# Seven quarter products in place of eight in twenty MLP blocks of a decoder layer, with the MLP input normalised first and the residual kept in HBM

## The chip, the core and the metric

The kernel runs on one NeuronCore of a Trainium2 chip. A core has five engines with a queue each: TensorE (PE in the profile; its weight loads are PEld), VectorE (DVE), ScalarE (ACT), GpSimd (POOL) and SyncE (SP), which here only issues DMAs. Each engine runs its queue in order; semaphores tie the queues together. The metric is the device time of one execution in microseconds (us).

## What is computed

One inference step of a hybrid decoder layer: a token mixer (gated linear attention and retention), a cross-attention into 256 memory tokens, and a squared-ReLU MLP, each between two RMSNorms and added to the residual. There are 576 tokens (512 of a prompt, 64 of samples), the width is 1024, the MLP's hidden width 4096, and all is in 32-bit floats. What the change touches is the end of `layer`:

```python
x = x + rmsnorm(cross_attn(rmsnorm(x, g_pre_xa), mem_k, mem_v, w_xq, w_xo), g_post_xa)
hf = rmsnorm(x, g_pre_ffn)
x = x + rmsnorm(jnp.square(jax.nn.relu(hf @ w_up)) @ w_down, g_post_ffn)
```

## The kernel before

Activations lie transposed: features on the 128 partitions (8 tiles of 128 for the width, `KT`), tokens along the free dimension, 576 columns (`NT`) in two halves of 288 (`NH`). A 32-bit product is made of three matmuls in the fp32r type (`mm3`): every operand is split into a rounded high part and the rest (`split`: an ACT cast for the high part, a DVE subtraction for the rest; `split_p` has the subtraction on POOL). So each matmul of 128 x 128 weights against 288 columns stands three times: high weight by high input, rest by high, high by rest.

Weights come from HBM in tiles of 128 x 1024 (512 KB, one output tile of 128 features). `plan` lists them in the order of use; `wfetch` issues the next DMA on SP into one of four `wraw` buffers, `wsplit` makes `wh` and `wl` of it (three buffers each), `wnext` hands out a split tile and keeps two ahead. `gemm_m` takes one tile through both halves (48 matmuls) into a PSUM tile of `psg` (two buffers).

The MLP runs in four groups `g` of 1024 hidden features. An up stage (eight `gemm_m`) gives the hidden features, which ACT (relu), DVE (square) and a split turn into the operand `xh`, `xl` of the down stage (eight more), whose sums collect in `y3` on DVE. In group 0's up stage and in group 3's down stage the halves run one after the other (`project`), and four of the eight weight tiles are kept from the first half to the second (`KEEP_FFN`), so that two are loaded again.

What stands around: `chain_xa` ends the cross-attention. As a generator it goes on by one step at each `tick`, between the matmuls of a `project`: `residual` norms the projection, adds it into `res` (which stays in SBUF to the end) and writes `res` times the gain, split, to `bh`, `bl`. The MLP's input is thus not yet divided by its root mean square; its statistics (`vff`) enter only at the end, in `rstd` of the last `residual`, which adds the MLP's normed output to `res` and stores it to `y_out`. The order on each engine is that of the built program; a scheduler places the instructions of the generators and of neighbouring stages.

```python
for g in range(4):
    ...
        for k in range(KT):
            to_h(h2(hh[:, k, :]), h2(hl[:, k, :]), gemm_m(fh, fl))
    ...
        for k in range(KT):
            ps = gemm_m(hh, hl)
            ...
                nc.vector.tensor_tensor(out=h2(y3[:, k, :]), in0=ps, in1=h2(y3[:, k, :]), op=ALU.add)
```

Of the kernel before, what the change touches and what calls it, by code (L numbers as in the profile page):

```python
# [56 lines left out]
def decoder_step(ctx, tc, xT, memT, ktc, vc, s_gla, s_ret, w_in, w_ga, w_a2, w_mix, w_xq, w_xk, w_xv, w_xo,  # L57
                 w_up, w_down, vecs, cst, gam, y_out, mk_out, mv_out, sg_p, sr_p, sg_s, sr_s):
# [20 lines left out]
    vff = [[perm.tile([96, 3], F32, name=f"vff{i}{j}") for j in range(2)] for i in range(2)]  # L79
# [5 lines left out]
    wz = acta.tile([P, 256], F32R, name="wz")  # L85
# [75 lines left out]
    for g in range(4):  # L161
        plan += keep(whole(w_up), KEEP_FFN) + rest(whole(w_up), KEEP_FFN) if g == 0 else whole(w_up, 4 * g)
        plan += keep(whole(w_down, 12), KEEP_FFN) + rest(whole(w_down, 12), KEEP_FFN) if g == 3 else whole(w_down, 4 * g)
    raws, ready, staying = [], [], []

    def wfetch():
        if plan:
            src, mode = plan.pop(0), RING
            if isinstance(src, tuple):
                src, mode = src  # L170
            raw = wp.tile([P, 1024], F32, name="wraw", bufs=N_RAW)
            nc.sync.dma_start(out=raw if len(src.shape) == 2 else raw.rearrange("p (k n) -> p k n", n=src.shape[2]), in_=src)
# [29 lines left out]
    def gemm(ps, w, xh, xl, c, k0=0, k1=KT):  # L202

        wh, wl = w
        for k in range(k0, k1):
            mm3(ps, wh[:, k, :], wl[:, k, :], xh[:, k, c], xl[:, k, c], k == 0, k == KT - 1)

    def gemm_m(xh, xl):
# [5 lines left out]
        return ps[:, :, :NH]  # L214

# [152 lines left out]
    y2p = ctx.enter_context(tc.tile_pool(name="y2p", bufs=1))  # L368
# [51 lines left out]
    def residual(y, r, half, ss, ss2=None, g2=None, oh=None, ol=None, scale=None, done=None):  # L420

        c = hc(half)
        rs, dg = rstd(ss, 3, 96, scale)
        yield
        bc = bcast(dg, 3, 96)
        for j in range(4):
# [81 lines left out]
    fh = actb.tile([P, KT, NT], F32R, name="bh")  # L508
    fl = actb.tile([P, KT, NT], F32R, name="bl")

    def chain_xa(half):

        ss2 = y2p.tile([P, 2, 384], F32, name="ss2")
        yield from residual((y2a, y2b)[half], rr, half, ss[half], ss2[:, :, :NH], V_PRE_FFN, fh, fl)

        def stats():
            yield
            nc.vector.reciprocal(vff[half][0], meansq(ss2[:, :, :NH], 3, 96))
            nc.vector.tensor_tensor(out=vff[half][1], in0=vff[half][0], in1=vff[half][0], op=ALU.mult)
        yield from stats()  # L520

    side.append(chain_xa(0))
    project(ah, al, 1, to(y2b, V_POST_XA, ss[1]))
    drain()
    side.append(chain_xa(1))


    hp = ctx.enter_context(tc.tile_pool(name="hp", bufs=2))
    staying.append(ctx.enter_context(tc.tile_pool(name="keepf", bufs=KEEP_FFN)))
    y3 = None  # L530
    for g in range(4):
        hh = acta.tile([P, KT, NT], F32R, name="xh")
        hl = acta.tile([P, KT, NT], F32R, name="xl")

        def to_h(hv, lv, ps):
            r = hp.tile([P, 2, NH], F32, name="hr")
            nc.scalar.activation(r, ps, AF.Relu)  # L537
            nc.vector.tensor_tensor(out=r, in0=r, in1=r, op=ALU.mult)  # L538
            split(hv, lv, r)

        if g == 0:
            for half in range(2):
                c = hc(half)
                project(fh, fl, half, lambda b, ps, first: to_h(hh[:, 2 * b:2 * b + 2, c], hl[:, 2 * b:2 * b + 2, c], ps), keep=KEEP_FFN)
                drain()
        else:
            for k in range(KT):
                to_h(h2(hh[:, k, :]), h2(hl[:, k, :]), gemm_m(fh, fl))
        if g == 0:
            y3 = biga.tile([P, KT, NT], F32, name="y3", tag="biga")  # L550
        if g < 3:
            for k in range(KT):
                ps = gemm_m(hh, hl)
                if g == 0:
                    nc.scalar.copy(h2(y3[:, k, :]), ps)
                else:
                    nc.vector.tensor_tensor(out=h2(y3[:, k, :]), in0=ps, in1=h2(y3[:, k, :]), op=ALU.add)  # L557

    def last(half):
# [672 lines left out]
```

## Time and profile before

| | |
|---|---|
| median of 3 runs (lowest, highest) | 1225.04 us (1223.53, 1228.98) |
| the profiled execution | 1223.69 us, its span 1222.0 us |
| busy share of the span | PE 98%, DVE 57%, ACT 43%, POOL 13% |
| matmuls | 9194 |
| mean granted TensorE clock | 0.991 of 2.4 GHz |

The span reaches from the first to the last instruction. A matmul's record lasts about 0.3 us, but they are pipelined: the step from one to the next is what counts. Idle time of an engine that nobody waits for costs nothing. Waits are given with the instruction that ended them, under its engine, its line in the kernel and the tile it writes and reads.

### The profile page before, as it was taken

How to read it: one execution, taken by the hardware profiler on the slowest of the kernel's cores; microseconds unless marked ns; L12 is line 12 of the kernel's file. 1: busy time of each engine (PE TensorE's matmuls, PEld its weight loads, DVE VectorE, ACT ScalarE, POOL GpSimd, SP SyncE). 2: the span in 40 equal slices, each digit the busy share in tenths (PEclk: the TensorE clock that was granted, in tenths of full speed). 3: DMA queues.
4: the chain of work that ended last, by engine and by line, in shares of the span. 5: the costliest groups of instructions: out<-in, count | busy, mean ns of one | idle time of the engine just before them, and what ended most of it. 6: DMA issues, size and time to landing. Idle time of an engine off the chain costs nothing.

```text
span 1222.0 us, 22137 instructions
## 1 busy us (share of the span) xinstructions
PE 1193.4 (98%) x9194; PEld 1170.8 (96%) x9194; DVE 692.9 (57%) x1217; ACT 527.9 (43%) x944; POOL 155.2 (13%) x156
## 2 busy tenths in 40 slices
PE   8999999999999999999999999999999999999995
PEld 8999999999999999999999777999999999999995
DVE  6757667566757675768576443783224324333544
ACT  6634556544544354535564444653223213213431
POOL 1521213121312231221001000000000000000000
PEclk9999999999999999999999999999999999999997
DMA  8753423242424242423644767442222222222401
GB/s 278 242 177 103 124 82 116 86 126 87 125 72 128 84 126 71 141 86 112 207 150 135 247 218 242 155 139 70 86 73 84 87 87 86 75 82 87 139 11 67
DMA packets 60372, 149.45 MB, mean 122 GB/s; under 512 B 5520, under 2 KB 30224, under 8 KB 60144
## 3 DMA queue, kind: packets, MB, share of 16 engines
q1 hardware_dynamic: 60272, 148.04, 37.9%
q8 instruction: 72, 1.18, 0.4%
q14 instruction: 28, 0.23, 0.1%
HBM read 134.12 MB, written 13.89 MB: 121 GB/s over the span
## 4 chain that ended last, share of the span: by engine, by line
PE 93%; DMA 2%; ACT 2%; DVE 2%; issue 1%; POOL 0%; SPq 0%; POOLq 0%; DVEq 0%; ACTq 0%
PE psg L198 27%; PE psg L200 27%; PE psg L199 27%; PE psa L198 2%; PE psa L200 1%; PE psa L199 1%; PE pso L1056 1%; DMA wraw<-in_w_xo 1%; PE psa L223 1%; ACT wh L92 1%; PE psa L773 1%; PE pso L899 1%; PE pso L900 1%; PE psa L901 1%; PE psa L776 1%; PE psa L833 1%
## 5 line engine op out<-in xcount | busy, mean ns | idle before, releaser
L198 PE MATMUL psg<-xh,wh 128*128 128x288 f32 x1808 | 537.1, 297 | 3.8 <-ACT wh L92 3.1
L199 PE MATMUL psg<-xh,wl 128*128 128x288 f32 x1808 | 533.5, 295 | 2.6 <-DVE wl L93 2.6
L200 PE MATMUL psg<-xl,wh 128*128 128x288 f32 x1808 | 532.8, 295 | 0.0
L198 PEld LDWEIGHTS psg<-xh,wh 128*128 128x128 f32 x1808 | 339.8, 188 | 6.6 <-ACT wh L92 5.1
L199 PEld LDWEIGHTS psg<-xh,wl 128*128 128x128 f32 x1808 | 340.0, 188 | 3.7 <-DVE wl L93 3.5
L200 PEld LDWEIGHTS psg<-xl,wh 128*128 128x128 f32 x1808 | 339.5, 188 | 0.8 <-DVE xl L93 0.8
L93 DVE TENSOR_TENSOR wl<-wraw,wh 128x1024 fp32r<-128x1024 f32 x189 | 233.2, 1236 | 105.2 <-ACT wh L92 104.3
L92 ACT CAST wh<-wraw 128x1024 fp32r<-128x1024 f32 x189 | 197.9, 1050 | 173.2 <-PE psg L200 122.8
L198 PE MATMUL psg<-bh,wh 128*128 128x288 f32 x640 | 189.4, 296 | 1.1 <-DMA wraw<-out_mk 1.1
L200 PE MATMUL psg<-bl,wh 128*128 128x288 f32 x640 | 188.7, 295 | 0.0
L199 PE MATMUL psg<-bh,wl 128*128 128x288 f32 x640 | 188.6, 295 | 0.0
L198 PEld LDWEIGHTS psg<-bh,wh 128*128 128x128 f32 x640 | 120.1, 188 | 1.8 <-ACT wh L92 1.3
L199 PEld LDWEIGHTS psg<-bh,wl 128*128 128x128 f32 x640 | 120.1, 188 | 0.3 <-DVE wl L93 0.2
L200 PEld LDWEIGHTS psg<-bl,wh 128*128 128x128 f32 x640 | 120.1, 188 | 0.2 <-DVE bl L93 0.2
L236 POOL TENSOR_TENSOR rs<-ms,mhalf 96x3 f32<-96x3 f32 (+1 forms) x9 | 8.9, 987 | 537.3 <-DVE ms L235 408.5
L538 DVE TENSOR_TENSOR hr<-hr 128x576 f32<-128x576 f32 x32 | 24.3, 758 | 90.0 <-ACT hr L537 90.0
L537 ACT ACTIVATE hr<-psg 128x576 f32<-128x576 f32 x32 | 20.9, 652 | 106.9 <-PE psg L200 106.9
L557 DVE TENSOR_TENSOR y<-psg,y 128x576 f32<-128x576 f32 x16 | 12.1, 758 | 62.7 <-PE psg L200 62.7
L759 ACT COPY vt<-psg 128x512 f32<-128x512 f32 x16 | 9.4, 588 | 78.0 <-PE psg L200 78.0
L688 POOL TENSOR_TENSOR rs<-mv,mhalf 128x1 f32<-128x1 f32 (+1 forms) x40 | 26.9, 672 | 108.4 <-DVE mv L683 60.7
L258 DVE TENSOR_TENSOR ss<-ss,sq 128x576 f32<-128x576 f32 x34 | 26.3, 773 | 16.8 <-ACT sq L257 16.7
L761 DVE COPY vd<-psg 128x96 f32<-128x96 f32 x32 | 6.7, 252 | 51.0 <-ACT vt L759 51.0
(274 smaller groups left out, 1605.8 us busy)
## 6 DMA issues: line engine op xcount, KB each, us to landing
wraw<-in_w_in SPq DMA_DIRECT2D x64, 512.0 KB, 3.6
wraw<-in_w_up SPq DMA_DIRECT2D x34, 512.0 KB, 3.6
wraw<-in_w_down SPq DMA_DIRECT2D x34, 512.0 KB, 3.6
wraw<-in_ktc SPq DMA_DIRECT2D x16, 512.0 KB, 4.0
wraw<-in_vc SPq DMA_DIRECT2D x16, 512.0 KB, 5.4
wraw<-in_w_xq SPq DMA_DIRECT2D x14, 512.0 KB, 4.4
wraw<-in_w_xo SPq DMA_DIRECT2D x14, 512.0 KB, 4.6
wraw<-in_w_mix SPq DMA_DIRECT2D x12, 512.0 KB, 4.5
```

Source lines behind the costliest of these rows:

```text
L92: nc.scalar.copy(hi, src)
L93: nc.vector.tensor_tensor(out=lo, in0=src, in1=f32(hi), op=ALU.subtract)
L198: nc.tensor.matmul(out, ah, bh, start=first, stop=False)
L199: nc.tensor.matmul(out, al, bh, start=False, stop=False)
L200: nc.tensor.matmul(out, ah, bl, start=False, stop=last)
L223: nc.tensor.matmul(ps[:t, i:i + 1], ss[:, l, i * t:(i + 1) * t], ones[:, 0:1], start=l == 0, stop=l == ls - 1)
L258: eng.tensor_tensor(out=ss, in0=ss, in1=sq[:, :, :n], op=ALU.add)
L537: nc.scalar.activation(r, ps, AF.Relu)
L538: nc.vector.tensor_tensor(out=r, in0=r, in1=r, op=ALU.mult)
L688: nc.gpsimd.tensor_tensor(out=rs[:t], in0=mv[:t], in1=mhalf[:t, 0:1], op=ALU.pow)
L773: nc.tensor.matmul(sc[:, :P], kf[:, ci], qf[:, ci], start=True, stop=True)
L776: nc.tensor.transpose(tp[:, P + m * P:P + (m + 1) * P], vt[:, m, ci], ident)
```

## The change

A block is two output tiles (256 features) against 1024 inputs and all 576 tokens. Groups 1 to 3 up and groups 1 and 2 down have 20 of them. Each operand is seen as 2 x 2 quarters: the weights by output tile and by even or odd input tile, the activations by even or odd input tile and by half of the tokens. Winograd's form of Strassen's scheme needs seven products of quarters (12 matmuls each) and sums of quarters ahead of and behind them. `sevenfold` issues the seven products. The sums on the output side lie in two PSUM accumulators, `acc` and the halves `b`, `c` of a `psg` tile: a product is added onto what is there, and the sum is read off in between by functions given to it (`p1`, `p5`, `u2`, `c11`, `c22`, `c12`, `c21`: ACT copies or DVE adds into `hr` for an up block, DVE adds into `y3` for a down block). The sums of weight quarters are made on POOL in `begin` (four subtractions of 128 x 512 per block), and 3.5 tiles per block are split instead of two (`unit_a` to `unit_d`; the last is the half tile `wdh`, `wdl`). The sums of activation quarters are made in `sums_f` (once, on POOL) for the up blocks and in `pairs` (one subtraction on POOL, three on DVE, for each block) for the down blocks.

For this the MLP's input is normed before it is split (`chain_xa` goes through a second `rstd`); `res` is written to `y_out` (`spill`), its SBUF room goes to `y3`, and it is read back into `res2` before the last stage. `KEEP_FFN` is gone: six tiles instead of two are loaded and split again in each of the two `project` pairs. The square of the hidden features is on ACT for the most part.

```diff
+        def unit_a():
+            pair(p0)
+            wfetch()
+        def unit_c():
+            minus(qt[:, 0], q1[:, 1], q0[:, 1])
+            pair(t)
+        def unit_b():
+            pair(p1)
+        def unit_d():
+            minus(q1[:, 0], q1[:, 0], qt[:, 0])
+            dh, dl = (wdp[0].tile([P, 512], F32R, name=n) for n in ("wdh", "wdl"))
+            split(dh, dl, q1[:, 0])
+            ready.append((dh, dl))
+        minus(qt[:, 1], q1[:, 1], q0[:, 1])
+        minus(q0[:, 1], q0[:, 1], q0[:, 0])
+        units.extend([unit_a, unit_c, unit_b, unit_d])
+        wfetch()
...
+        wa = ready.pop(0)
+        wsplit()
+        prod(acc, wa, 0, "A11", True)
+        p1(acc)
+        if raws and raws[0][1] == SEVEN:
+            begin()
+        prod(c, wa, 1, "S1", True)
+        p5(c)
+        wc = ready.pop(0)
+        prod(acc, wc, 0, "S2", False)
+        u2(acc)
+        wsplit()
+        wb = ready.pop(0)
+        prod(b, wb, 0, "A12", True)
+        c11(b)
+        prod(acc, wc, 1, "S3", False)
+        c22(acc)
+        wsplit()
+        prod(c, wb, 1, "S4", False)
+        c12(c)
+        wd = ready.pop(0)
+        if units:
+            wsplit()
+        prod(acc, wd, 0, "A22", False)
+        c21(acc)
...
+    def pairs(c1, c2, sh, sl, e1):
...
+        nc.gpsimd.tensor_tensor(out=c2[:, 0], in0=c1[:, 0], in1=c2[:, 0], op=ALU.subtract)
+        e1.tensor_tensor(out=c1[:, 0], in0=c2[:, 1], in1=c1[:, 0], op=ALU.subtract)
+        e1.tensor_tensor(out=c1[:, 1], in0=c1[:, 1], in1=c1[:, 0], op=ALU.subtract)
+        split(sh[:, 2:4], sl[:, 2:4], c2)
+        split(sh[:, 0:2], sl[:, 0:2], c1)
...
+    res2 = fsp.tile([P, KT, NT], F32, name="res2", tag="fsh")
+    for half in range(2):
+        for k in range(0, KT, 2):
+            nc.sync.dma_start(out=res2[:, k:k + 2, hc(half)], in_=y_out[:, k:k + 2, hc(half)])
```

How the rows move on an engine is shown at three places. First VectorE in the up stage of group 1, where `wl` is the rest of a weight tile and `hr`, `xl` the hidden features: before, for two of the output tiles,

```order
L538 TENSOR_TENSOR hr_11058<-hr_11058 128x576
L93 TENSOR_TENSOR wl_11126<-wraw_11003,wh_11125 128x1024
L93 TENSOR_TENSOR xl_10882<-hr_11058,xh_10881 128x576
L538 TENSOR_TENSOR hr_11118<-hr_11118 128x576
L93 TENSOR_TENSOR wl_11186<-wraw_11063,wh_11185 128x1024
L93 TENSOR_TENSOR xl_10882<-hr_11118,xh_10881 128x576
```

The same place now, from the square `c21` of one block (L740) to the sum `c12` of the next (the last L725); `fh`, `ha` and `hh` are the operands of the down stage:

```order
L740 TENSOR_TENSOR hr_11135<-hr_11135 128x288
L659 TENSOR_TENSOR hr_11135<-hr_11135 128x288
L93 TENSOR_TENSOR wdl_11277<-wraw_11054,wdh_11276 128x512
L93 TENSOR_TENSOR ha_10987<-hr_11134,ha_10987 128x2x288
L662 TENSOR_TENSOR hr_11134<-hr_11135,hr_11134 128x288
L93 TENSOR_TENSOR hl_10986<-hr_11135,hh_10985 128x2x288
L663 TENSOR_TENSOR hr_11134<-hr_11134 128x288
L93 TENSOR_TENSOR wl_11325<-wraw_11159,wh_11324 128x1024
L93 TENSOR_TENSOR hl_10986<-hr_11134,hh_10985 128x2x288
L725 TENSOR_TENSOR hr_11271<-psg_11274,hr_11271 128x288
L725 TENSOR_TENSOR hr_11272<-psa_11273,hr_11272 128x288
L93 TENSOR_TENSOR wl_11362<-wraw_11293,wh_11361 128x1024
```

Six rows for two output tiles have become fifteen: these twelve, and behind them one more L725, one `wl` and the split of `fh`.

Second VectorE in the down stage of group 1: before, for two output tiles and the next weight tile,

```order
L93 TENSOR_TENSOR wl_11478<-wraw_11363,wh_11477 128x1024
L557 TENSOR_TENSOR y3_10432<-psg_11425,y3_10432 128x576
L93 TENSOR_TENSOR wl_11534<-wraw_11419,wh_11533 128x1024
L557 TENSOR_TENSOR y3_10432<-psg_11481,y3_10432 128x576
L93 TENSOR_TENSOR wl_11590<-wraw_11475,wh_11589 128x1024
```

and now, one block, in which the third L753 is `u2`:

```order
L753 TENSOR_TENSOR y3_10483<-psa_11781,y3_10483 128x288
L93 TENSOR_TENSOR wdl_11785<-wraw_11600,wdh_11784 128x512
L753 TENSOR_TENSOR y3_10483<-psg_11782,y3_10483 128x288
L93 TENSOR_TENSOR wl_11833<-wraw_11686,wh_11832 128x1024
L753 TENSOR_TENSOR y3_10483<-psa_11781,y3_10483 128x288
L753 TENSOR_TENSOR y3_10483<-psg_11782,y3_10483 128x288
L753 TENSOR_TENSOR y3_10483<-psa_11781,y3_10483 128x288
L93 TENSOR_TENSOR wl_11866<-wraw_11801,wh_11865 128x1024
L753 TENSOR_TENSOR y3_10483<-psg_11782,y3_10483 128x288
L93 TENSOR_TENSOR wl_11883<-wraw_11718,wh_11882 128x1024
L753 TENSOR_TENSOR y3_10483<-psa_11781,y3_10483 128x288
```

Two sums read off PSUM have become seven, and the rest of the next block's first weight tile (`wl_11833`) stands ahead of `u2`.

Third GpSimd, which before had nothing in these groups; now, in one up block of group 1, with the subtractions of two weight blocks (`wraw_11156` is the buffer of sums):

```order
L212 TENSOR_TENSOR wraw_10933<-wraw_10933,wraw_11019 128x512
L212 TENSOR_TENSOR wraw_11156<-wraw_11054,wraw_11022 128x512
L212 TENSOR_TENSOR wraw_11022<-wraw_11022 128x512
L661 TENSOR_TENSOR hr_10989<-hr_10988,hr_10989 128x288
L212 TENSOR_TENSOR wraw_11156<-wraw_11054,wraw_11022 128x512
L212 TENSOR_TENSOR wraw_11054<-wraw_11054,wraw_11156 128x512
```

The first and the last row here are `unit_d` of two consecutive blocks. `unit_d` overwrites half of a tile that `unit_b` splits, so it waits for that tile's `wl` on VectorE.

## Rows read from the trace of the kernel before

**Rows 1.** The page, part 1: busy us (share) and instructions of each engine.

```profile
PE 1193.4 (98%) x9194; PEld 1170.8 (96%) x9194; DVE 692.9 (57%) x1217; ACT 527.9 (43%) x944; POOL 155.2 (13%) x156
```

**Rows 2.** The page, part 4: the chain that ended last, shares by engine.

```profile
PE 93%; DMA 2%; ACT 2%; DVE 2%; issue 1%; POOL 0%; SPq 0%; POOLq 0%; DVEq 0%; ACTq 0%
```

**Rows 3.** Windows: length, busy PE, PEld, DVE, ACT, POOL, clock, DMA share, GB/s.

```profile
780.00:820.00 40.00, 40.00 (x315) 39.75 (x314) 38.11 (x60) 27.98 (x45) 1.78 (x1) 1.00 0.48 154
...
900.00:1000.00 100.00, 100.00 (x755) 99.79 (x754) 36.34 (x39) 25.40 (x32) 0.00 (x0) 1.00 0.27 84
```

**Rows 4.** Timeline of ACT, up stage of group 1: start us, duration us, instruction, idle before.

```profile
937.38 0.65 ACT L537 ACTIVATE hr<-psg 128x576 f32<-128x576 f32 x1 [4.20 <-PE psg L200]
...
943.74 0.66 ACT L537 ACTIVATE hr<-psg 128x576 f32<-128x576 f32 x1 [4.20 <-PE psg L200]
```

**Rows 5.** Groups by shape, from 775 us on: count, busy us, mean ns, idle before.

```profile
L93 DVE TENSOR_TENSOR wl<-wraw,wh 128x1024 fp32r<-128x1024 f32 x72 | 88.1, 1225 | 62.8 <-ACT wh L92 62.8
...
L577 DVE TENSOR_TENSOR ss<-ss,sq 128x288 f32<-128x288 f32 x4 | 1.8, 459 | 2.0 <-ACT sq L576 2.0
L575 DVE TENSOR_TENSOR y<-psg,y 128x288 f32<-128x288 f32 x4 | 1.8, 458 | 6.1 <-PE psg L200 6.1
...
L92 ACT CAST wh<-wraw 128x1024 fp32r<-128x1024 f32 x72 | 75.3, 1048 | 102.9 <-PE psg L200 91.0 <-DMA wraw<-in_w_down 9.2 <-DMA wraw<-in_w_up 2.7
```

**Rows 6.** Timeline of DVE: two instructions back to back.

```profile
1009.15 1.23 DVE L93 TENSOR_TENSOR wl<-wraw,wh 128x1024 fp32r<-128x1024 f32 x1 [0.17 <-ACT wh L92]
1010.29 0.75 DVE L93 TENSOR_TENSOR xl<-hr,xh 128x576 fp32r<-128x576 f32 x1
```

**Rows 7.** Groups by shape on POOL, whole span.

```profile
L942 POOL TENSOR_TENSOR G<-G,t 128x576 f32<-128x576 f32 x14 | 20.1, 1436 | 19.9 <-ACT t L941 19.9
...
L97 POOL TENSOR_TENSOR ql<-t,qh 128x512 fp32r<-128x512 f32 x4 | 5.2, 1296 | 7.7 <-ACT qh L96 7.7
```

**Rows 8.** Tile xn on POOL: ns least/median/most, first and last start.

```profile
L97 POOL TENSOR_TENSOR xl<-xn,xh x16: 803/818/1894, 29.3 to 59.8; 128x288 fp32r<-128x288 f32 x16
```

**Rows 9.** Timeline of DVE and POOL where both work at once, in the mixer.

```profile
80.85 1.23 DVE L93 TENSOR_TENSOR wl<-wraw,wh 128x1024 fp32r<-128x1024 f32 x1
80.90 2.46 POOL L703 TENSOR_TENSOR t<-t,t 128x576 f32<-128x576 f32 x1 [7.82 <-DVE t L702]
...
85.28 1.29 POOL L97 TENSOR_TENSOR ql<-t,qh 128x512 fp32r<-128x512 f32 x1 [1.92 <-ACT qh L96]
...
85.38 1.28 DVE L740 TENSOR_TENSOR qblk<-t,qblk 128x64 fp32r<-128x64 f32 x1 [0.70 <-ACT qblk L739]
...
125.92 1.43 POOL L942 TENSOR_TENSOR G<-G,t 128x576 f32<-128x576 f32 x1 [1.20 <-ACT t L941]
...
126.47 0.42 DVE L814 SCALAR_TENSOR_TENSOR T<-T,psa 128x256 f32<-128x256 f32 x1 [1.17 <-PE psa L200]
```

**Rows 10.** Timeline of DVE where the first half's residual begins.

```profile
774.17 1.42 DVE L429 TENSOR_TENSOR y2a<-y2a,psa 128x576 f32<-128x576 f32 x2 [1.08 <-PE psa L247]
```

**Rows 11.** DMA issues: line, engine, count, KB each, median us to landing.

```profile
wraw<-in_w_down SPq DMA_DIRECT2D x34, 512.0 KB, 3.6
...
xr<-in_xT SPq DMA_DIRECT2D x8, 288.0 KB, 4.1
```

**Rows 12.** Groups by shape from 775 us on, the late statistics.

```profile
L238 DVE TENSOR_TENSOR rs<-rs,vff 96x3 f32<-96x3 f32 x2 | 0.3, 158 | 2.0 <-POOL rs L236 2.0
```

**Rows 13.** Timeline of PE at a wait for weights.

```profile
754.34 0.40 PE L198 MATMUL psg<-xh,wh 128*128 128x288 f32 x1 [1.08 <-ACT wh L92]
755.60 0.61 PE L199 MATMUL psg<-xh,wl 128*128 128x288 f32 x1 [0.86 <-DVE wl L93]
...
756.25 0.44 PE L198 MATMUL psg<-xh,wh 128*128 128x288 f32 x1
756.49 0.44 PE L199 MATMUL psg<-xh,wl 128*128 128x288 f32 x1
```

**Rows 14.** Windows behind that wait (columns as in Rows 3).

```profile
756.00:760.00 4.00, 4.00 (x22) 4.00 (x22) 0.00 (x0) 0.00 (x0) 0.00 (x0) 0.64 0.91 324
```

More of the change, by code (lines that the diff above doesn't have):

```diff
@@ L214, in gemm_m, with sevenfold, prod @@
         return ps[:, :, :NH]
+    def sevenfold(x, p1, p5, u2, c11, c22, c12, c21):
+        def prod(out, w, q, a, first):
+            wh, wl = (v.rearrange("p (q k n) -> p q k n", k=4, n=P) for v in w)
+            for k in range(4):
+                xh, xl = x(a)
+                for i, (s, m) in enumerate(((wh, xh), (wl, xh), (wh, xl))):
+                    nc.tensor.matmul(out, s[:, q, k], m[:, k], start=first and k == i == 0, stop=k == 3 and i == 2,
+                                     skip_group_check=True)
+            tick()
+        while len(ready) < 3:
+            wsplit()
+        acc = atile()[:, :NH]
+        ps = gtile()
+        b, c = ps[:, 0, :NH], ps[:, 1, :NH]
+        wa = ready.pop(0)
[3 more added lines that the diff above has]
+        if raws and raws[0][1] == SEVEN:
+            begin()
+        prod(c, wa, 1, "S1", True)
[13 more added lines that the diff above has]
+        wd = ready.pop(0)
+        if units:
+            wsplit()
+        prod(acc, wd, 0, "A22", False)
+        c21(acc)
     def meansq(ss, n, t, eps=EPS):
@@ L418, in rr, with residual @@
         return res[:, kk, c]
[L420 removed]
+    def residual(y, r, half, ss, ss2=None, g2=None, oh=None, ol=None, done=None, eng=nc.vector, res=res):
         c = hc(half)
[L423 removed]
+        rs, dg = rstd(ss, 3, 96)
         yield
@@ L522, in decoder_step, with quarters, x @@
[L522 to L529, printed above, removed]
+    fh = actb.tile([P, 4, 4, NH], F32R, name="fh", tag="bh")
+    fl = actb.tile([P, 4, 4, NH], F32R, name="fl", tag="bl")
+    def quarters(h, l):
+        def x(k, c):
+            q = (2 if c.start else 0) + k % 2
+            return h[:, q, k // 2], l[:, q, k // 2]
+        return x
@@ new lines, in sums_f, with xf7 @@
+    def sums_f():
+        for j in range(4):
+            c1, c2 = (hp.tile([P, 2, NH], F32, name="hr") for _ in range(2))
+            for i, c in enumerate((c1, c2)):
+                q = slice(2 * i, 2 * i + 2)
+                nc.gpsimd.tensor_tensor(out=c, in0=f32(fh[:, q, j]), in1=f32(fl[:, q, j]), op=ALU.add)
+            yield
+            pairs(c1, c2, fsh[:, :, j], fsl[:, :, j], nc.gpsimd)
+            yield
+    SQ = {"S2": 0, "S4": 1, "S3": 2, "S1": 3}
+    def xf7(n):
+        return (fsh[:, SQ[n]], fsl[:, SQ[n]]) if n in SQ else tuple(
+            t[:, {"A11": 0, "A12": 1, "A22": 3}[n]] for t in (fh, fl))
@@ L545, in decoder_step @@
+                project(ff, None, half, to_h)
                 drain()
-        else:
+            y3 = bigb.tile([P, KT, NT], F32, name="y3", tag="res")
+            side.append(sums_f())
             for k in range(KT):
[L548 to L555, printed above, removed]
-                else:
-                    nc.vector.tensor_tensor(out=h2(y3[:, k, :]), in0=ps, in1=h2(y3[:, k, :]), op=ALU.add)
+                nc.scalar.copy(h2(y3[:, k, :]), gemm_m(quarters(hh, hl), None))
+                tick()
```

182 lines of the change are left out of this document (136 added, 46 removed).

## The prediction, made before the changed kernel had run

> **What bounds the kernel now.** The page first: PE is busy for 98% of the span, no other engine for more than 57% [rows 1], and 93% of the chain that ended last is PE [rows 2]. So an edit is worth what it takes from PE or adds to PE's waits. Then the windows of the MLP, since an average hides stages: from 900 to 1000 us PE has no gap, with DVE busy for 36 of 100 us and POOL for none; from 780 to 820 us, where the cross-attention's residual runs, DVE is at 38 of 40 us [rows 3]. The reader is to see that the MLP has room on the side engines, and that the stretch ahead of it has none. The rate: one evicted tile follows the other after 943.74 - 937.38 = 6.36 us [rows 4], and that is 48 matmuls, 0.1325 us each. A block of two tiles (96 matmuls) takes 12.72 us; 20 blocks 254.4 us. The sum below is made against the profiled execution, 1223.69 us (1222.0 of span and 1.7 around it), which lies 1.35 us under the median of the three runs.
>
> **Taken off PE.** Seven products of 12 are 84 matmuls: 84 x 0.1325 = 11.13 us a block, 1.59 us less. Twenty times that is 31.8 us, and if nothing else became late the time would be 1192 us. The question is whether the side engines deliver a block in 11.13 us.
>
> **What DVE and POOL need for a block.** DVE: 1.225 us for the rest of a 1024-wide tile, 0.459 us for 288 columns in SBUF, 0.458 us where one operand is in PSUM [rows 5]. Back to back it starts every 1.14 us after a 1024 [rows 6], 0.09 less than the duration; by the same subtraction I take 0.38 for 288, 0.67 for 576 and 0.60 for 512 columns (estimates from these rows). POOL: 1.296 us for 512 columns, 1.436 for 576 [rows 7], 0.82 for 288 [rows 8].
>
> The two don't run side by side; three places in the mixer show it [rows 9]. A POOL operation of 576 columns (1.436 us alone) that starts 0.05 us behind a `wl` takes 2.46 us, until 1.28 us after the `wl` has ended. A DVE operation of 64 columns, begun 0.1 us behind a POOL operation of 512, takes 1.28 us, to 0.09 us past POOL's end. And a DVE operation with one operand in PSUM goes through in 0.42 us in the middle of a POOL operation. So with two operands in SBUF on DVE, one of the two stands still until the other is done; about 0.15 us of a delayed POOL operation is hidden (1.436 - 1.28). The Trainium skill says the same (SBUF — State Buffer, "Who interferes with whom"): a DVE instruction with two SBUF inputs and a GpSimd instruction that reads SBUF exclude each other for their full length, and it speaks against this change; by its "full length" an up block below would take 15.1 us instead of 14.2, which the 0.15 us of those rows does not bear out.
>
> An up block of groups 1 and 2 costs DVE 3 x 1.14 + 0.60 + 3 x 0.67 + 8 x 0.38 = 9.07 us, and POOL 4 x (1.296 - 0.15) + 0.67 = 5.25 us. In the built order DVE has, behind `wl` of `unit_b`, nothing but SBUF work until `c11`, and POOL begins its five operations with just that `wl`; the three adds out of PSUM come when POOL is through. So the two run in turn: 9.07 + 5.25 = 14.3, I take **14.2 us** (floor 13.2 if all three PSUM adds fell under POOL, ceiling 9.07 + 4 x 1.296 + 0.82 = 15.1 with nothing hidden). PE waits in it for `u2` (ACT stands behind the cast that waits for POOL's L661) and for `c22`. The first block of a group has no sums of its own kind behind it (11.2 us), the second some (13.3 us): 11.2 + 13.3 + 2 x 14.2 = 52.9 us against 4 x 12.72 = 50.9, **+2.0 us** in each of two groups.
>
> By the Trainium skill (GPSIMD Engine Reference, "3.1 Elementwise — side-by-side cycle accounting") a GpSimd add of 2048 columns takes 4497 ns, an estimate of 1.12 us for 512; the row's 1.296 us decides. With the page's figure the steady up block would be 13.5 us.
>
> A down block costs DVE 6.7 us, POOL 4.6; there is room, but a chain closes. After `wl` of `unit_b`: 0.1 to POOL; `unit_d` 1.3; the next tile's first subtraction 1.3; `wdl` slips in, 0.6; the second 1.15; the ACT cast 1.05 [rows 5]; `wl` of `unit_a`, held until POOL's third is through, 1.3; then `u2`, which stands behind that `wl` on DVE, 0.46. That is 7.26 us, and only then may S3 write `acc`, which without a wait would be due 6.36 us into the block. From S3 it goes on: two products 3.18, an eviction 0.15 + 0.4, `wl` of `unit_b` 1.2, and the round is closed: 7.26 + 4.93 = **12.2 us**. Bounds: 11.13 (nothing late) and 12.9 (each POOL step 0.15 longer). The first down block also waits for the last up block's sums: `ha` leaves DVE about 7.4 us after the up block's last product, the last `hl` after 12.3, while PE has 18 matmuls (2.4 us) that need neither; S3 to A22 follow, 17.7 us in all (bounds 13 and 19). 17.7 + 3 x 12.2 = 54.3: **+3.4 us**, twice.
>
> Group 3's up blocks have no `pairs`: DVE 6.9 us, POOL 4.6 in turn, and the chain through `u2` is late in every other block: 11.2 + 3 x 11.7 = 46.3, **-4.6 us** (bounds -6.4 and -1).
>
> **Ahead of group 1.** The first half's chain now has two rounds of statistics. PE meets the second sum of squares 116 matmuls (15.4 us) into the projection, near 782.4 us (it began 48 matmuls ahead of 774.17 [rows 10], near 767); DVE's share of it (4 + 4 + 3 steps of 0.67 and two `wl`, 9.65 us, from 774.17) ends near 783.9. **+1.5 us.** In group 0's up stage the same for the second half, with the additions on POOL (4 x 1.43) in turn with DVE: **+3 us** (0 to 6). In group 0's down stage POOL makes all of `sums_f`: 8 x 1.436 + 16 x 0.82 = 24.6 us, some of it only when the buffers of the up stage come free; ACT's casts of these sums stand ahead of the first two copies out of `psg`, which PE needs for its third and fourth tile. **+4 us** (0 to 6). The four weight tiles loaded and split once more in each of the two `project` pairs (4 x 1.14 us of DVE, 4 x 1.05 of ACT in 25 us of matmuls) lie in stages in which DVE is free for most of the time, as in the second window of [rows 3]: nothing; without that cover it would be 4.6 us each.
>
> **At the end.** `res2` puts 8 loads of 288 KB ahead of the sixth weight tile on SP. Such a load lands after 4.1 us, a weight tile after 3.6 [rows 11]; 2.4 MB and 0.5 MB at the 324 GB/s of [rows 14] are 9 us, and the tile is due 15.9 us into the stage: covered, at most +2 if the queue is slower. The late statistics lose three small DVE steps like the 0.158 us of [rows 12]: **-0.5 us**.
>
> **Sum.** 2 x 2.0 + 2 x 3.4 - 4.6 + 1.5 + 3 + 4 - 0.5 = +14.2 us: 1237.9 in a profiled execution, **1239 us** beside the median.
>
> **The rivals.**
> *PE stays the bound.* If POOL's steps found DVE on PSUM or waiting for something else, S3 would start on time and every block take 11.13 us: -31.8, with 5 of the 8.5 us ahead of group 1 left: 1198 us. For it: DVE's own work is below 11.13 us in every block, and ACT's too. Against it: the built order, in which the POOL steps begin with a DVE row and meet SBUF work. It decides at `u2`: done by 6.4 us after a block's first product, the change is faster.
> *The shared stretch is shorter than I count.* Up blocks at 13.2, down at 11.6, the first down block at 14: 2 x (2 x 1.0 + 0.7) + 2 x 3 x 0.6 + 2 x 3.7 = 16.4 us less than mine, 1222 us, no change. For it: the scheduler may have left POOL free stretches that I don't see; against it, the order of DVE's rows.
> *The clock falls.* At 754 us PE waited 1.08 and 0.86 us within 2 us, and the next window's granted clock is 0.64 of 2.4 GHz [rows 13, 14], so part of it was at 1.2 GHz, a matmul every 0.24 instead of 0.13 us [rows 13]. An up block would have two waits of that size. If half of the eight up blocks and both transitions lose 12 matmuls' worth twice (2 x 12 x 0.11 = 2.6 us), it is +16: 1255 us. Against it: DVE and POOL, not PE, would carry these blocks, and part of it would hide. The Trainium skill (TensorE: Matmul & The Clock Gate, "What's actually happening") says that the lower clock is the default and activity releases it; how long a wait must be, no row here shows.
>
> **How the numbers follow.** The forecast has a chance of 0.55 (1226 to 1252), the first rival 0.2 (1193 to 1206), the second 0.1 (1214 to 1230), the clock 0.15 (1248 to 1268). The range that leaves out no more than a part of the first and the end of the last is 1199 to 1262. About 0.5% (6 us) is what a measurement can tell from no change: below 1219 the first rival and some of the second, 0.24; within, the rest of the second and the forecast's lower end, 0.16; above 1231, 0.60.
>
> **What would show it.** In the changed kernel's trace: the start of consecutive blocks 14 us apart in the up stages of groups 1 and 2, 12 in their down stages, 11.7 in group 3; POOL's subtractions well over 1.3 us and some `wl` over 1.23 us, in turn; PE's waits put down to `hr` and `y3` (`u2`, `c22`), not to weights; a wait of some 5 us at each change from up to down. It would be wrong if blocks come every 11.1 us, if PE waits for `wh`, `wl` or a DMA instead, or if the largest loss lies ahead of group 1.

## The result, and the profile after

The changed kernel takes 1276.42 us (median of 4 runs, 1272.72 to 1278.25) against 1225.87 for the kernel before beside it: 1.0407 times as long, 95% interval 1.0382 to 1.0431. The forecast was 1239 us, its range 1199 to 1262. The sign was right, the size was not: +50 us instead of +14. The profiled execution took 1272.72 us, 1271.0 of them span. One of the four executions with the idle load below took 2287.63 us, the other three 1263.93 to 1265.03, and it is left out of the comparison.

The changed kernel's page, the busy row of part 1, the first row of part 4 (the chain that ended last) and one group of part 5:

```profile
PE 1186.6 (93%) x8958; PEld 1151.0 (91%) x8958; DVE 831.3 (65%) x1357; ACT 610.4 (48%) x1088; POOL 331.5 (26%) x282
...
DVE 7%; PE 7%; issue 5%; POOL 5%; ACT 3%; POOLq 0%; DVEq 0%; ACTq 0%
...
L212 POOL TENSOR_TENSOR wraw<-wraw 128x512 f32<-128x512 f32 x80 | 114.7, 1434 | 188.3 <-DVE wl L93 184.3
```

Against [rows 1, 2], PE has gone from 98% to 93% of the span, and the chain, which was 93% PE, can be followed for a part of the span only and mixes DVE, PE, POOL and ACT. L212 is the line of the weight sums: 80 on POOL, four in each of 20 blocks. What PE waited for, over the whole span (us in total, times, longest):

```profile
PE psg L286 <- ACT hr L746: 10.4, 6, 1.7
PE psa L286 <- DVE y L753: 10.1, 6, 1.7
PE psg L257 <- DVE wl L93: 7.0, 8, 2.2
PE psg L286 <- ACT hh L92: 6.1, 2, 3.0
...
PE psg L256 <- ACT y L712: 4.7, 2, 2.4
...
PE psg L286 <- DVE hr L725: 4.1, 5, 0.8
PE psa L286 <- ACT hr L747: 3.4, 3, 2.4
```

L286 is the sevenfold product, L256 to L258 the plain one. L746 (`p1`, `p5`), L747 (`u2`) and L725 (the sums) read it off in up blocks, L753 in down blocks. The losses lie in all stages but the last two, as the first matmul of each stage in the two traces tells (a table of my own; the last column is the prediction's term):

| stage | before, us | after, us | difference | predicted |
|---|---|---|---|---|
| second half of the cross-attention output | 40.0 | 42.2 | +2.2 | +1.5 |
| group 0, up | 53.5 | 60.5 | +7.1 | +3 |
| group 0, down (with `sums_f`) | 51.1 | 60.7 | +9.5 | +4 |
| group 1, up | 50.9 | 60.9 | +10.1 | +2.0 |
| group 1, down | 51.1 | 59.0 | +7.8 | +3.4 |
| group 2, up | 50.9 | 58.1 | +7.3 | +2.0 |
| group 2, down | 51.1 | 60.1 | +8.9 | +3.4 |
| group 3, up | 50.9 | 48.5 | -2.4 | -4.6 |
| group 3, down, and the end | 68.1 | 68.4 | +0.3 | -0.5 |

With 1.8 us by which the first of these stages began earlier, that is +49.0 us of span. Every term but the last, which is nearly nothing, has the predicted sign, and every one came out worse than predicted. In blocks: a steady up block takes 15.2 us in group 1 and 15.4 to 15.6 in group 2 (14.2 predicted), the second block of either group 15.4 (13.3), a steady down block 13.2 (12.2), the first up block of group 1 15.2 and of group 2 11.8 (11.2), the first down blocks 19.4 and 20.5 (17.7), group 3's up blocks 11.6 to 12.6 (11.7 but for the first).

### The profile page after: what moved, and what is told of

It is laid out like the page before. It is cut to its first block, busy times and chain, and to the rows that moved or that the text cites. A ratio compares the mean times of both kernels' runs of the same rounds, so it can differ in the third digit from the quotient of the medians.

```text
span 1271.0 us, 22266 instructions
## 1 busy us (share of the span) xinstructions
PE 1186.6 (93%) x8958; PEld 1151.0 (91%) x8958; DVE 831.3 (65%) x1357; ACT 610.4 (48%) x1088; POOL 331.5 (26%) x282
## 3 DMA queue, kind: packets, MB, share of 16 engines
q8 instruction: 70, 1.15, 0.4%
## 5 line engine op out<-in xcount | busy, mean ns | idle before, releaser
L256 PE MATMUL psg<-xh,wh 128*128 128x288 f32 x1296 | 386.2, 298 | 3.5 <-ACT wh L92 3.5
L257 PE MATMUL psg<-xh,wl 128*128 128x288 f32 x1296 | 382.9, 295 | 3.6 <-DVE wl L93 3.6
L258 PE MATMUL psg<-xl,wh 128*128 128x288 f32 x1296 | 382.6, 295 | 0.0
L256 PEld LDWEIGHTS psg<-xh,wh 128*128 128x128 f32 x1296 | 243.9, 188 | 5.9 <-ACT wh L92 5.5
L257 PEld LDWEIGHTS psg<-xh,wl 128*128 128x128 f32 x1296 | 243.9, 188 | 4.9 <-DVE wl L93 4.7
L258 PEld LDWEIGHTS psg<-xl,wh 128*128 128x128 f32 x1296 | 243.8, 188 | 0.0
L212 POOL TENSOR_TENSOR wraw<-wraw 128x512 f32<-128x512 f32 x80 | 114.7, 1434 | 188.3 <-DVE wl L93 184.3
L256 PE MATMUL psg<-hh,wh 128*128 128x288 f32 x256 | 77.6, 303 | 5.4 <-ACT y L712 4.7
L258 PE MATMUL psg<-hl,wh 128*128 128x288 f32 x256 | 77.2, 302 | 1.0 <-DVE hl L93 1.0
L257 PE MATMUL psg<-hh,wl 128*128 128x288 f32 x256 | 76.8, 300 | 0.3 <-DVE wl L93 0.3
L256 PEld LDWEIGHTS psg<-hh,wh 128*128 128x128 f32 x256 | 49.5, 193 | 6.3 <-ACT y L712 5.2
L891 POOL TENSOR_TENSOR rs<-mv,mhalf 128x1 f32<-128x1 f32 (+1 forms) x40 | 26.8, 670 | 108.7 <-DVE mv L886 60.9
L258 PEld LDWEIGHTS psg<-hl,wh 128*128 128x128 f32 x256 | 49.3, 193 | 1.5 <-DVE hl L93 1.5
L258 PE MATMUL psg<-fl,wh 128*128 128x288 f32 x128 | 38.0, 297 | 1.6 <-POOL fl L97 1.6
```

Of the source, the lines that this page charges most:

```text
L212: nc.gpsimd.tensor_tensor(out=out, in0=a, in1=b, op=ALU.subtract)
L256: nc.tensor.matmul(out, ah, bh, start=first, stop=False)
L257: nc.tensor.matmul(out, al, bh, start=False, stop=False)
L258: nc.tensor.matmul(out, ah, bl, start=False, stop=last)
L891: nc.gpsimd.tensor_tensor(out=rs[:t], in0=mv[:t], in1=mhalf[:t, 0:1], op=ALU.pow)
```

## What POOL's sums do to DVE

DVE and POOL by shape in three up blocks of group 1 (931.2 to 976.9 us) of the changed kernel: count, busy us, mean ns, idle before:

```profile
L93 DVE TENSOR_TENSOR wdl<-wraw,wdh 128x512 fp32r<-128x512 f32 x3 | 5.3, 1774 | 0.0
L740 DVE TENSOR_TENSOR hr<-hr 128x288 f32<-128x288 f32 x3 | 4.7, 1553 | 0.0
...
L659 DVE TENSOR_TENSOR hr<-hr 128x288 f32<-128x288 f32 x3 | 4.3, 1422 | 0.1
...
L93 DVE TENSOR_TENSOR ha<-hr,ha 128x576 fp32r<-128x576 f32 x3 | 4.0, 1340 | 0.0
...
L663 DVE TENSOR_TENSOR hr<-hr 128x288 f32<-128x288 f32 x3 | 1.3, 445 | 0.0
...
L212 POOL TENSOR_TENSOR wraw<-wraw 128x512 f32<-128x512 f32 x12 | 17.8, 1482 | 23.9 <-DVE wl L93 23.5
```

L740, L659 and L663 each have two operands of 288 columns in SBUF and so the same amount of work. L663 runs when POOL is silent and takes 0.445 us, the other two meet a POOL sum and take 1.42 and 1.55. The timeline of POOL in one of these blocks (start, duration, and in brackets the idle time before and who ended it):

```profile
962.80 4.30 POOL L212 TENSOR_TENSOR wraw<-wraw 128x512 f32<-128x512 f32 x3 [7.93 <-DVE wl L93]
967.06 1.24 POOL L661 TENSOR_TENSOR hr<-hr 128x288 f32<-128x288 f32 x1
968.26 1.79 POOL L212 TENSOR_TENSOR wraw<-wraw 128x512 f32<-128x512 f32 x1
```

POOL is silent for 7.93 us while DVE works, then runs for 7.25 us (962.80 to 970.05) while DVE gets one operation through for each of POOL's, five in all. The sum is the block, 15.2 us.

## Experiments

**The sums left out, and the sums on DVE.** Theory 1: POOL's sums set the blocks, because POOL and DVE keep each other waiting (the expectations call it the port that the two share). Theory 2: TensorE waits because the two halves of one `psg` tile (the accumulators `b` and `c`) are held as one. The trace gives theory 2 the waits behind L746 and L725: A12 goes into `b`, but waits for the copy of `c`, and S4 goes into `c`, but waits for the sum in `b`. The first kernel leaves out the four sums and loads the third tile `t` instead, so its output isn't the layer's; the second has one word changed:

```
-            nc.gpsimd.tensor_tensor(out=out, in0=a, in1=b, op=ALU.subtract)
+            nc.vector.tensor_tensor(out=out, in0=a, in1=b, op=ALU.subtract)
```

Without the sums: 

> The changed kernel with the four sums over weights of each sevenfold block left out (the third tile is loaded from HBM instead, so every cast, subtraction and product stays; its output isn't the reference's). In the changed kernel an up block of groups 1 and 2 takes 15.2 us, a down block 13.2, where its 84 matmuls are 11.1. Theory 1, POOL's sums and the port that POOL and DVE share set the blocks: up falls to about 11.6, down to 11.2, group 3's up from 12.1 to 11.2, so 1272.7 - 8 x 3.6 - 8 x 2.0 - 4 x 0.9 = about 1224 us. Theory 2, TensorE waits because the two halves of one psg tile are held as one (the second product into it waits for the copy of the first): up stays over 14, down 13.2, so over 1262.

With the sums on DVE: 

> The four sums of each sevenfold block on DVE instead of POOL (some 0.62 us each, half of the 1.23 of a 1024 subtraction, so 2.5 us more of DVE in a block). Theory 1 (POOL and the shared port): up 15.2 to about 13.0 (DVE's 14.0 less some 3.5 of waiting for POOL, plus 2.5), down 13.2 to 11.2 (DVE about 9.2), so 1272.7 - 8 x 2.2 - 8 x 2.0 = about 1239 us. Theory 2 (the psg halves) or a DVE that is already full: up 15.2 to 17 since DVE has more, down 13.2 as before: 1272 to 1287.

Measured: 1233.9 us without them, 1233.34 with them on DVE (ratio to before 1.0071, 1.0045 to 1.0096). So 42 or 43 of the 50 us go with one word, and theory 2 as the main cause (over 1262 us in both) is out. Blocks with the sums on DVE: three steady up blocks 12.0 on average, steady down 11.2, group 3's 11.2 to 11.7. The 1239 us expected were a little too many. Without the sums the 1224 us expected were missed by 10: down blocks are 11.2 as well, but up blocks 12.7, not 11.6. There ACT's casts come so early that `p1`'s copy stands behind the cast of `hh`, which waits 0.91 us for POOL's L661. Three up blocks with the sums on DVE (931.8 to 967.7 us):

```profile
L212 DVE TENSOR_TENSOR wraw<-wraw 128x512 f32<-128x512 f32 x12 | 8.2, 682 | 0.0
...
L659 DVE TENSOR_TENSOR hr<-hr 128x288 f32<-128x288 f32 x3 | 1.4, 450 | 0.0
...
L740 DVE TENSOR_TENSOR hr<-hr 128x288 f32<-128x288 f32 x3 | 1.3, 449 | 0.0
...
L661 POOL TENSOR_TENSOR hr<-hr 128x288 f32<-128x288 f32 x3 | 3.5, 1160 | 72.1 <-DVE hr L659 72.1
```

A sum costs DVE 0.68 us, POOL took 1.48, and L659 and L740 are back at 0.45. The page's busy row shows that DVE's busy time is no longer for 80 more instructions: 831.5 us against 831.3.

```profile
PE 1182.3 (96%) x8958; PEld 1153.5 (94%) x8958; DVE 831.5 (67%) x1437; ACT 610.5 (50%) x1088; POOL 216.7 (18%) x202
```

**Exclusion or latency.** A sum on POOL is also slower by itself, and casts wait for it. To tell the two apart the sums stay on DVE, and POOL gets four subtractions of the same size per block into a scratch tile:

```
+        def load(a):
+            s = npool.tile([P, 2, NH], F32, name="sq", bufs=1).rearrange("p a n -> p (a n)")[:, :512]
+            nc.gpsimd.tensor_tensor(out=s, in0=a, in1=a, op=ALU.subtract)
...
+            load(q1[:, 1])
```

> The kernel with the four weight sums on DVE (1233.3 us), and POOL given four subtractions of the same size per block again, at the same places, whose results go to a scratch tile that nobody reads. It tells the port from the latency. If what a sum on POOL costs is that DVE and POOL shut each other out: DVE's busy time rises by about the 53 us that 80 sums of 0.66 us added and the freed port gave back, up blocks go from 12.0 to 14 or 15, down blocks from 11.2 to 12.5, 1233 + 8 x 2.5 + 8 x 1.3 + 4 = about 1267 us. If it is that the casts have to wait for POOL's slower result (1.4 us against 0.66): nobody waits for these, and it stays at 1231 to 1236.

> The sums on DVE and the same number of POOL subtractions into a tile that nobody reads, for a trace of its blocks. If DVE and POOL shut each other out of a port, DVE's two-operand subtractions in the up blocks last 1.3 to 1.8 us where they meet POOL's and 0.45 to 0.75 where they don't, up blocks take 14 to 15 us, down blocks about 12.5, and the time is 1262 to 1268. If something else (a buffer held longer by POOL's read) makes the kernel slow, DVE's subtractions last 0.45 to 0.75 as without the load, and the waits stand at the casts of wh for a later transfer.

Measured: 1264.8 us, and 1267.71 for the same kernel in two more executions, of which the trace is one; 31 to 34 us over the 1233.3 without this idle load. Nobody waits for its results, so this cost isn't their latency. The load also holds the buffers of the weight tiles that it reads; no run separates what that adds, but in the three blocks below PE waits for copies, sums and `wl` alone, for no transfer. DVE is busy for 34 us more than without the load, with the same instructions (the page's busy row, then DVE and POOL in three up blocks, 935.6 to 979 us):

```profile
PE 1195.6 (94%) x8958; PEld 1161.2 (91%) x8958; DVE 865.5 (68%) x1437; ACT 613.2 (48%) x1088; POOL 327.5 (26%) x282
```

```profile
L93 DVE TENSOR_TENSOR wl<-wraw,wh 128x1024 fp32r<-128x1024 f32 x8 | 11.8, 1470 | 0.5 <-ACT wh L92 0.5
...
L748 DVE TENSOR_TENSOR hr<-hr 128x288 f32<-128x288 f32 x3 | 3.9, 1294 | 0.0
...
L667 DVE TENSOR_TENSOR hr<-hr 128x288 f32<-128x288 f32 x3 | 1.3, 446 | 0.0
...
L216 POOL TENSOR_TENSOR sq<-wraw 128x512 f32<-128x512 f32 x13 | 18.9, 1451 | 19.3 <-DMA wraw<-in_w_downs 9.4 <-DMA wraw<-in_w_ups 9.2
```

L216 is the load; L748 is the square that was L740. Which DVE operations get longer has moved with the place at which POOL's start: L748 meets them, L667 (the old L659) doesn't. These three up blocks take 14.5 us on average, steady down blocks 11.6 to 12.5, about what was expected if the two shut each other out. The changed kernel is another 9 to 12 us slower; I put that down to latency and order, and no run separates the two.

**The `psg` halves.** `b` and `c` get a tile each, in the changed kernel, with the sums on DVE, and with all of POOL's tensor work on DVE (the last is described below):

```
-        ps = gtile()
-        b, c = ps[:, 0, :NH], ps[:, 1, :NH]
+        b, c = gtile()[:, 0, :NH], gtile()[:, 1, :NH]
```

> The accumulators b and c of a sevenfold block in two psg tiles instead of the two halves of one, nothing else. Theory 2: the waits of 1.7 us ahead of A12 and of 0.8 ahead of S4 go, with the slow pace after them, so up 15.2 to about 12.6, down unchanged at 13.2: 1272.7 - 8 x 2.6 = about 1252 us. Theory 1: the waits only move to the next result that DVE and POOL owe (DVE's 14.0 us and POOL's 7.1 in a block stay), up 14.5 to 15.2: 1267 to 1273.

> The four sums on DVE, and the accumulators b and c in two psg tiles. With the sums on DVE an up block of groups 1 and 2 takes 12.0 us and DVE is busy 11.2 to 11.9 of them; PE's 84 matmuls are 11.1. If the two halves of one psg tile are the bound that is left: up 12.0 to 11.3, 8 x 0.7 = 5.6 less than the 1233.3 us of the kernel with the sums on DVE, about 1228. If DVE's own work is: up 11.8 to 12.0, 1231 to 1234.

> The kernel with all of POOL's tensor work moved to DVE, and b and c in two psg tiles. If the psg halves are the bound left in up blocks: 5.6 us under the same kernel without (about 1212 where that is 1217). If DVE's work is: the same within 2 us.

Measured: 1270.77 (5.7 less, intervals overlap), 1229.84 (3.5 less, intervals overlap), 1211.07 (6.2 less than 1217.25, intervals apart). In the changed kernel the up block only goes from 15.2 to 14.4 us, and the time lies in theory 1's range: the waits ahead of A12 and S4 are gone, and PE waits instead for ACT's copies `p1` and `u2`, 2.4 us a block, which stand behind casts that wait for POOL. With POOL silent the same edit takes 1 us from each up stage of groups 1 and 2 and 1.4 from each first down block. So theory 2 is true of a second limit, and worth some 6 us, not 43.

**Ahead of group 1.** Plain blocks in the changed kernel's frame price the norm, the spilled residual and the dropped kept tiles; and two edits move what else the change gave POOL: `sums_f` with its pairs, then L661, the residual adds of the second half and the low parts of the normalised input.

```
-                nc.gpsimd.tensor_tensor(out=c, in0=f32(fh[:, q, j]), in1=f32(fl[:, q, j]), op=ALU.add)
+                nc.vector.tensor_tensor(out=c, in0=f32(fh[:, q, j]), in1=f32(fl[:, q, j]), op=ALU.add)
...
-            pairs(c1, c2, fsh[:, :, j], fsl[:, :, j], nc.gpsimd)
+            pairs(c1, c2, fsh[:, :, j], fsl[:, :, j], nc.vector)
...
-            split_p(fh[:, q, j], fl[:, q, j], xn)
+            split(fh[:, q, j], fl[:, q, j], xn)
...
```

Plain blocks: 

> The changed kernel with every MLP block as eight products of the old kind (no sums over weights or activations at all), but with the input normalised first, the residual in HBM, no kept tiles in the MLP. It prices what comes ahead of group 1 and at the end. Theory: normalising first costs what the trace of the changed kernel shows in the last half of the cross-attention output and in group 0's up half (2.2 + 7.1 us, less 1.8 by which these start earlier) and 0.3 at the end: 1225.9 + 7.8 = about 1234 us; then sums over activations and sevenfold blocks are the other 39. Rival: the losses in group 0's up half come from something else (a POOL that the later sums queue on), and this is 1226 to 1228.

Plain blocks again, a single execution: 

> The changed kernel with plain blocks once more (1237.7 us): one look for the spread of that kernel, whose time without the sums is what normalising first, the residual in HBM and the dropped kept tiles cost. 1232 to 1240 us, 7 to 15 over the kernel before.

`sums_f` on DVE: 

> The four sums on DVE, and the sums over the MLP input during group 0's down stage on DVE too (the adds, the pairs). In the kernel with only the weight sums moved that stage takes 60.6 us, 51.1 in the kernel before; PE waits there twice, 2.2 and 4.0 us, for y copies on ACT that stand behind casts of these sums, and its clock falls after. Theory 1: the casts are late because POOL's sums are (1.43 us an op, 2 us when DVE is between): 60.6 to about 52, so about 1225 us. Rival: ACT's queue has the casts ahead of the copies whoever makes the sums, and DVE's pairs wait for casts in turn: 58 to 61, 1231 to 1234.

All of it on DVE: 

> As before it, and the rest of the tensor work that the change put on POOL moves to DVE as well: the subtraction in each set of pairs, the residual adds of the second half and the low parts of the normalised input. Theory 1: group 0's up half, 62 us with the weight sums moved (53.5 in the kernel before; wl 2.4 us instead of 1.2 where POOL is running), falls to about 55; the blocks stay, the change from up to down loses 0.5 each: 1225 - 7 - 1 = about 1217 us. Rival: DVE, busy 41 of those 62 us, is then too full for the weights to be in time, and group 0's up half stays at 60 or more: 1225 or over.

Plain blocks with the norm's part on DVE: 

> Plain blocks everywhere in the changed kernel's frame, with the residual adds of the second half and the low parts of the normalised input on DVE instead of POOL. The same frame with them on POOL takes 1237.7 us (group 0's up half 60.5). If POOL's work is what normalising first costs: 60.5 to about 56 as in the sevenfold kernel with all on DVE, 1232 to 1234; what the sevenfold blocks bring at their best is then 1233 - 1211 = 22 of the 31.8 us that TensorE saves. If the second norm's own chain is: 1236 to 1239.

Measured: plain 1237.74 (1.0089, 1.0063 to 1.0115) and 1234.83; `f_dve` 1223.05, 10.3 less than with the weight sums alone on DVE; `all_dve` 1217.25, another 5.8 less; plain with the norm on DVE 1230.35 (1.0041, 1.0024 to 1.0057). So what comes ahead of group 1 costs 11 to 13 us without any sevenfold block, and 6 to 7 of that are POOL's work (the two plain kernels compared by their ratios or by their medians); 4 to 5 us are left for the norm's own chain and the rest of the frame. Group 0's down stage in the changed kernel and in `f_dve` (windows: length, busy PE, PEld, DVE, ACT, POOL, clock, DMA share, GB/s):

```profile
855.30:916.00 60.70, 54.97 (x387) 54.22 (x386) 22.88 (x18) 18.81 (x26) 29.05 (x24) 0.94 0.21 61
```

```profile
855.00:906.10 51.10, 51.10 (x386) 51.05 (x385) 27.84 (x40) 19.04 (x26) 5.04 (x4) 1.00 0.24 73
```

POOL was busy for 29 us there. DVE does all but L661 of it in 5 us more, PE has no gap left, and the stage is as long as in the kernel before.

**The change from up to down.** In the best kernel so far the first down blocks are the longest. A12, which needs no sum, goes to second place (and its weights are split second), and then the first half of `ha` is made on its own. The first edit, cut:

```
+        if early:
+            wb = ready.pop(0)
+            prod(b, wb, 0, "A12", True)
+            c11(b)
         prod(c, wa, 1, "S1", True)
```

> The kernel with all of POOL's tensor work on DVE and two psg tiles (1211.1 us), and in the first down block of groups 1 and 2 the product A12, which needs no sum over activations, moved to second place, ahead of S1 and S2. These two blocks take 15.5 and 17.3 us where the others take 11.2; PE waits there for the last up block's ha and hh and its clock falls. If hh (the pairs) is what is late: 1.6 us of work fill the wait, and the clock stays up some more, 2 to 4 us each, 1203 to 1207. If ha, which A11 and A12 both need, is: the wait only moves, 1209 to 1212.

> The same, and in the last up block the first half of ha (A11's) is made as soon as its sum is there instead of together with the second, so that the chain behind S4 is on 288 columns instead of 576. If ha's chain is late: 1 us or more less at each of the two changes, 1 to 3 us under the kernel with A12 moved alone. If ACT's and DVE's six shorter instructions delay others as much as they shorten the chain: no difference.

Measured: 1211.41 and 1211.42, no difference from 1211.07. The longest wait that is left at the first change is 1.0 us for `ha` in the one and 1.8 for `hh` in the other. The two blocks take 15.6 us each in the first kernel, 16.1 and 15.9 in the second, 15.4 and 17.2 without either edit. At the first change the wait only moves; the 1.6 us that the second seems to gain are less than these times can tell (their intervals are 2 to 3 us to either side). What would shorten it isn't known.

**A version that beats both.** All the tensor work that the change gave POOL on DVE, and two `psg` tiles: 1211.07 us, 0.9887 of the kernel before (0.9867 to 0.9907). Three up blocks and the three steady down blocks of group 1 in it (same columns):

```profile
917.50:952.60 35.10, 34.74 (x256) 33.97 (x255) 33.96 (x59) 25.62 (x47) 0.00 (x0) 1.00 0.25 77
...
968.10:1001.10 33.00, 33.00 (x249) 33.00 (x249) 28.01 (x46) 11.37 (x12) 0.00 (x0) 1.00 0.33 102
```

POOL does nothing, PE has next to no gap, and DVE is busy for 34 of 35 us in up blocks: by that it would be the next bound, which no run tests. Against plain blocks in the same frame (1230.35) the sevenfold blocks bring 19 of the 31.8 us that they take off PE.

## Why the prediction was right in its sign and wrong in its size

In all the span grew by 49.0 us where the sum had 14.2. The mechanism came true; what failed are steps of it, and they are named term by term.

*PE's saving and what bounds a block: right.* 84 matmuls take 11.2 us in blocks where nothing is late. DVE and POOL in turn set the others, and PE waits in them for evictions, not for weights, as written. In up blocks they aren't the evictions that were named. `u2` and `c22` were to be late; what PE waits for in the three up blocks from 931.2 us on is `p5` ahead of A12 (1.7 us a block), `p1` ahead of S2 (0.7) and the sum `c11` ahead of S4 (0.8):

```profile
PE psg L286 <- ACT hr L746: 5.2, 3, 1.7
PE psg L286 <- DVE hr L725: 2.4, 3, 0.8
PE psa L286 <- ACT hr L746: 2.1, 3, 0.8
```

```profile
968.33 0.67 ACT L92 CAST hh<-hr 128x576 fp32r<-128x576 f32 x1 [2.64 <-POOL hr L661]
968.91 0.39 ACT L746 COPY hr<-psg 128x288 f32<-128x288 f32 x1
```

ACT does stand behind the cast that waits for POOL's L661, as written, but that already holds up `p5`, and the prediction had no term for the two halves of a `psg` tile being held as one.

*The steady up block, +1.0 us on 14.2.* "The two run in turn: 9.07 + 5.25" is the step: the mechanism is right, its terms are not. Measured in turn are 7.93 and 7.25. POOL's operations come every 1.2 to 1.8 us; I had counted 1.15 for a sum (1.296 of [rows 7] less 0.15 that would hide), and three in a row take 4.30. On the other side five DVE operations (2.4 us by the estimates) fit beside POOL's and lengthen its stretch by 1.25 (7.25 against 4 x 1.296 + 0.82 = 6.0), so 1.2 us are hidden, where I had 0.75. What the sum had at nothing is DVE's own waiting: the other 6.7 us of DVE take 7.93, of which 0.94 us are waits for PE and for ACT's cast of `wh`. So 14.3 (which I had taken as 14.2) less 0.4 and with 1.3 more is the 15.2. The ceiling of 15.1, with nothing hidden, was nearer by luck: it leaves out about as much waiting as it overcounts. The Trainium skill (SBUF — State Buffer, "SBUF: two separate sides") says that whichever of the two starts first gets the pair of ports that they share for the whole instruction, and by such a rule I had worked out 15.1. The trace agrees in that DVE and POOL wait for each other, but not in the price of each instruction: a 288-column DVE operation between two of POOL's adds some 0.14 us to POOL's pace (4.30 / 3 against 1.296), not its own 0.38.

*The steady down block, +1.0 us on 12.2.* The chain up to `u2` was 7.26 us in the prediction and is 7.2 in the trace (POOL's first sum at 1010.57, `u2` done at 1017.76). The way back, 4.93, is 5.95 (S3 at 1004.62 to 1010.57). The step that failed is that I had `wl` of `unit_b` follow the eviction; its cast has to go first, and waits until S4 has let go of the buffer. Timelines of PE, ACT, DVE and POOL:

```profile
1004.62 0.40 PE L286 MATMUL psa<-hh,wh 128*128 128x288 f32 x1 [1.67 <-DVE y L753]
```

```profile
1008.11 1.05 ACT L92 CAST wh<-wraw 128x1024 fp32r<-128x1024 f32 x1 [0.50 <-PE psg L286]
```

```profile
1009.20 1.23 DVE L93 TENSOR_TENSOR wl<-wraw,wh 128x1024 fp32r<-128x1024 f32 x1
```

```profile
1010.57 5.73 POOL L212 TENSOR_TENSOR wraw<-wraw 128x512 f32<-128x512 f32 x4 [7.45 <-DVE wl L93]
```

*The first blocks, +4.0 on 11.2 and +1.7 and +2.8 on 17.7.* I gave group 1's first up block no wait. It has one of 2.4 us: the copy for `u2` stands on ACT behind a cast that waits for POOL's third sum. The second up block, for which I had counted only some of the collision (13.3), has all of it (15.4). At the first change from up to down the waits sum to 4.7 us, near the 5 that were forecast. Behind such waits comes what the rival of the clock said, and it makes up 1.1 of the 1.7 us and 2.2 of the 2.8: PE's granted clock is 0.50 from 925 to 928 us and 0.51 from 986.5 to 989.5, the lower of its two levels, with a matmul every 0.24 us (two windows, then the timeline of PE).

```profile
925.00:928.00 3.00, 3.00 (x13) 3.00 (x14) 1.30 (x2) 0.00 (x0) 0.00 (x0) 0.50 0.36 97
986.50:989.50 3.00, 2.92 (x12) 2.92 (x13) 2.65 (x5) 1.60 (x2) 0.00 (x0) 0.51 0.00 0
```

```profile
984.18 0.61 PE L286 MATMUL psg<-hh,wh 128*128 128x288 f32 x1 [3.02 <-ACT hh L92]
...
987.23 0.44 PE L286 MATMUL psa<-hl,wh 128*128 128x288 f32 x1
987.47 0.44 PE L286 MATMUL psa<-hh,wh 128*128 128x288 f32 x1
```

From 750 us on there are seven such stretches against one before. At 0.107 us more for each of their 95 matmuls they cost 10.2 us, against 1.3: 9 of the 49. So that rival wasn't an alternative to the forecast but came on top of it; I had given it 15% as a case of its own. It isn't a cause by itself either: in `f_dve`, where the waits of group 0's down stage are gone, the clock there is 1.00.

*Ahead of group 1, +18.8 on +8.5 for the three stages.* The mechanism was named (ACT's casts of POOL's sums ahead of the copies out of `psg`), its size taken from the middle of a range of 0 to 6. The stage lost 9.5: waits of 2.3, 2.4 and 1.0 us, two stretches at the low clock, 1.4 to 1.5 us each. In group 0's up half it was the same exclusion: a `wl` waits out the last of POOL's residual adds, takes 2.42 us instead of 1.21, and PE waits 2.2 us for it (timelines of POOL and DVE). There I had looked only at the chain of the norm, not at the weights queued beside it.

```profile
804.83 6.68 POOL L530 TENSOR_TENSOR res<-y2b,res 128x576 f32<-128x576 f32 x4 [3.53 <-DVE y2b L529]
```

```profile
810.18 2.42 DVE L93 TENSOR_TENSOR wl<-wraw,wh 128x1024 fp32r<-128x1024 f32 x1
```

*The bounds, not only the values, were too narrow.* Six of the nine terms lie outside the range that their bounds gave. All six lie where POOL works beside DVE or PE meets new waits, and all erred the same way, though at different steps; a range that takes such terms as independent is too small. "If the largest loss lies ahead of group 1" was named as what would make it wrong: 18.8 of 49 lie there, the blocks have the larger part.

## What to carry to other kernels

Before giving POOL work to spare DVE, ask whether DVE has two-operand SBUF work at the same time. If it has, price POOL's operation at its full time on both engines: here the same subtraction costs 0.68 us on a DVE that is 67% busy, and 1.4 us on POOL, in which DVE gets through one operation of its own. Look at the halves of a shared accumulator tile and at ACT's queue only when that is settled. Allow for slow matmuls behind each new wait of 2 us: five of the six such waits in the MLP of the changed kernel had 10 to 21 of them.

## What the runs showed of the hardware that I had not expected

POOL's 512-column subtraction takes 1.296 us in the kernel before [rows 7] and comes every 1.43 us when DVE slips an operation in between; DVE's 0.45 us operation lasts 1.42 to 1.55 there, its 0.68 us one 1.77. In these blocks a row of DVE operations beside POOL so goes at one per POOL operation, whatever their size from 288 to 576 columns. And DVE's busy time hides this wait: it reads 831 us with the 80 sums on POOL and 831 with them on DVE.
